# The 90th head of a score kernel is laid out anew, and its store becomes three DMAs

## The chip, the cores and the metric

The kernel runs on one core of one Trainium2 chip. Times are microseconds of device time. The number that counts is the median of the runs; a profile of one more execution shows where the time goes. A core has engines that work side by side: PE (matrix products), DVE and ACT (elementwise work, here mostly copies), POOL (GpSimd) and SP, which in this kernel only issues DMAs. ACT and POOL can issue DMAs too. A DMA's bytes are moved by 16 DMA engines that all issuers share.

## The reference

```python
def setup_inputs():
    batch, n_heads, seq, head_dim = 8, 12, 1024, 64
    ...
def reference(q, k):
    return np.einsum('bhid,bhjd->bhij', q, k).astype(np.float32)
```

For each of 96 heads (8 batches of 12) the product of q (1024 x 64) with k transposed (64 x 1024) is written out as 1024 x 1024 numbers in float32. That is 4 MiB of output for each head and 403 MB in all, against 50 MB of input.

## The kernel before

The heads are worked in blocks of 2, 2, 4, 8, 8 and six times 12 heads (`sizes`). For a block, q and k are loaded (`Block.load`, L73, or head by head in `load_head`, L84), cast to half precision by POOL (`cast_rows`, L97, and `cast_quads`, L127), and transposed, so that the 64 numbers of a row lie along the partitions: by PE and a copy in the first two blocks (`transpose_rows`, L151 and L154), by DVE in the others (`transpose_quads`, L145). While one block's heads are computed, the next block is transposed and the one after that cast and loaded. The last block has no next one, so nothing of that kind lies beside its twelve heads, the 85th to the 96th.

`scores` computes one head. It takes an output tile `o_sb` of 128 partitions x 8 rows x 1024 numbers (32 KB per partition) from a pool of three buffers. Partition p holds rows 8p to 8p+7 of the result. In each of four steps PE makes two of these rows for all partitions: four products of 64 x 128 weights with 64 x 512 numbers of k (L171), into a PSUM tile of 128 x 2048. There are two such tiles. ACT copies each to `o_sb` (L181); only in the very first head, where the tiles are half as large, does DVE take every other copy (L179). After the fourth copy SP issues one DMA for the whole head (L185). It reads 32 KB from each of 128 partitions and writes 4 MiB to one stretch of memory.

A head's first copy has to wait until the store of three heads earlier has landed, since it takes over that store's buffer. PE fills the two PSUM tiles ahead of the copies. `pin` keeps all instructions of an engine in the order in which the program makes them, so the queues of PE, ACT, DVE, POOL and SP run as the code is written: SP's queue holds the stores one after another, ACT's the copies and, in earlier blocks, the loads.

`in_pool` has two buffers of 24 KB per partition that hold the loads of the larger blocks; `half_pool` has five small half-precision tiles. After the last block has been cast and transposed, neither pool is used any more.

Of the kernel before, what the change touches and what calls it, by code (L numbers as in the profile page):

```python
# [8 lines left out]
F16 = mybir.dt.float16  # L9
F32 = mybir.dt.float32  # L10
P = 128

@with_exitstack
def kernel(
# [6 lines left out]
    nc = tc.nc  # L21

    B, H, S, D = q.shape
    NT = S // P
    BH = B * H
# [5 lines left out]
    of = out.rearrange("b h i j -> (b h) i j")  # L31
# [3 lines left out]
    PE_BLOCKS = 2  # L35
    NMAX = max(sizes)
    CHUNK = 48 * 32

    consts = ctx.enter_context(tc.tile_pool(name="consts", bufs=1))
    ident = consts.tile([P, P], F16)  # L40

    in_pool = ctx.enter_context(tc.tile_pool(name="in_pool", bufs=2))
    half_pool = ctx.enter_context(tc.tile_pool(name="half_pool", bufs=5))
    tr_pool = ctx.enter_context(tc.tile_pool(name="tr_pool", bufs=2))
    out_pool = ctx.enter_context(tc.tile_pool(name="out_pool", bufs=3))

    pin = tc.keep_in_program_order

    def half_tile():
        half_sb = half_pool.tile([P, CHUNK], F16, tag="half")  # L50
        return half_sb

    class Block:
# [3 lines left out]
        def __init__(self, first, N, by_pe):  # L57
# [5 lines left out]
            self.halves = {}  # L63
            self.cut = max(1, self.R * 32 // CHUNK + (self.R * 32 % CHUNK > 0))

# [90 lines left out]
        def scores(self, n, side, ps_pool, w):  # L156
# [31 lines left out]
                )  # L188
            )

    blocks, first = [], 0
    for i, N in enumerate(sizes):
        blocks.append(Block(first, N, i < PE_BLOCKS))
# [4 lines left out]
    at = 0  # L198
# [13 lines left out]
    def next_load(eng):  # L212
        if stream:
            b, x = stream.pop(0)
            b.load(x, eng)
# [9 lines left out]
    def to_half(last):  # L225
        while casts:
            i, c = casts[0]
            if i > last or (blocks[i], c[0]) in stream:
                return
            blocks[i].cast_quads(*c)  # L230
            casts.pop(0)
# [6 lines left out]
    def block(i, heads, ps_pool, w):  # L238
        b = blocks[i]
        nxt = blocks[i + 1] if i + 1 < len(blocks) else None  # L240
        for n in heads:
            side = {}
            if nxt and nxt.by_pe:
                if n == 1:
                    side = {
                        u: [
                            lambda x=u // 2: nxt.transpose_rows(
                                x, ps_pool, nc.vector.tensor_copy
                            )
                        ]  # L250
                        for u in (1, 3)
                    }
            elif nxt:
                parts = nxt.chunks()
                some = [s for m, s in enumerate(parts) if m * b.N // len(parts) == n]
                side = {0: [lambda s=s: nxt.transpose_quads(*s) for s in some]}

            if n == LOADS.get(i, 6):
                side[1] = side.get(1, []) + [lambda: next_load(nc.scalar)] * 2
            b.scores(n, side, ps_pool, w)  # L260
            to_half(i + 2 + (n == b.N - 1))

    LOADS = {0: None, 1: None, 2: 1, 3: 4, 4: 4}
# [3 lines left out]
    with tc.tile_pool(name="first_pool", bufs=4, space=bass.MemoryType.PSUM) as pool:  # L267
        for x in range(2):
            blocks[0].transpose_rows(x, pool, (nc.vector.tensor_copy, nc.scalar.copy)[x])
        block(0, [0], pool, 1)  # L270
    po_pool = ctx.enter_context(
        tc.tile_pool(name="po_pool", bufs=2, space=bass.MemoryType.PSUM)
    )
    block(0, [1], po_pool, 2)
    for i in range(1, len(blocks)):
        if i + 1 < len(blocks):
            blocks[i + 1].alloc()
        block(i, range(blocks[i].N), po_pool, 2)
# [30 lines left out]
```

## Time and profile before

| | us |
|---|---|
| median of three runs | 1063.13 (1063.03 to 1064.67) |
| span of the profiled execution | 1061.8 |
| ACT busy in it | 697.6 |
| PE busy | 701.3 |
| DVE busy | 471.5 |
| POOL busy | 368.3 |
| one copy of 128 x 2048 by ACT | 1.860 |
| one product of 64 x 512 numbers by PE | 0.617 |

The span is the time from the first to the last instruction of the profiled execution. A page of the profile gives the busy time of the engines, the span in 40 slices, the DMA queues, the chain of work that ended last, the costliest groups of instructions by line, and the DMAs by the line that issues them. A busy share says little by itself: an engine that isn't on the chain can idle for nothing. The DMA row of the slices is the mean over all 16 DMA engines, so a slice in which one of them works alone looks almost empty. In the list of groups, "x96" counts instructions, and the number behind the bar is their total busy time, then the mean of one in nanoseconds.

### The profile page before, as it was taken

The page shows a single profiled execution, that of the slowest core. Times are in us where ns is not written, and L with a number is a line of the kernel's source. Part 1 is how long each engine was busy: PE and PEld are TensorE (multiplying, and loading weights), DVE is VectorE, ACT ScalarE, POOL GpSimd, SP SyncE. Part 2 cuts the span into 40 slices and gives each one's busy share as a digit, 9 for nine tenths or more (in the row PEclk, how much of TensorE's full clock was granted, in tenths as well). Part 3 has the DMA queues.
Part 4 walks back from the last instruction along what each step waited for, and adds up shares of the span by engine and source line. Part 5 has one row for each costly group of instructions (what it writes and reads, how often), then busy time and mean ns, then how long its engine had stood idle before and what let it go on. Part 6 is the DMA issues. An engine that isn't in the chain of part 4 may idle for free.

```text
span 1061.8 us, 4282 instructions
## 1 busy us (share of the span) xinstructions
PE 701.3 (66%) x1568; PEld 241.6 (23%) x1568; DVE 471.5 (44%) x75; ACT 697.6 (66%) x386; POOL 368.3 (35%) x286
## 2 busy tenths in 40 slices
PE   6866755755677367773677836777367777778770
PEld 2322211211222122221222212222122222222220
DVE  2999601991696007960079600795007950000000
ACT  4856745755777366774677746777467777777771
POOL 6959128607630463303733046330463200000000
DMA  9999999999999999999999999999999999999997
GB/s 385 428 429 435 433 431 435 435 422 440 428 430 432 432 430 432 435 422 429 431 433 431 415 436 431 433 435 422 428 434 435 434 432 432 434 433 427 434 431 311
DMA packets 17588, 453.25 MB, mean 427 GB/s; under 512 B 1952, under 2 KB 1952, under 8 KB 2976
## 3 DMA queue, kind: packets, MB, share of 16 engines
q1 hardware_dynamic: 14688, 406.85, 89.1%
q10 hardware_dynamic: 2880, 46.14, 10.4%
q8 instruction: 12, 0.20, 0.1%
q14 instruction: 8, 0.07, 0.0%
HBM read 50.33 MB, written 402.65 MB: 427 GB/s over the span
## 4 chain that ended last, share of the span: by engine, by line
DMA 70%; ACT 17%; PE 7%; DVE 2%; issue 1%; POOL 1%; ACTq 0%; SPq 0%
DMA out_dram<-o_sb 70%; ACT o_sb L181 17%; PE ps L171 7%; DVE qT L145 1%; DVE kT L145 1%; DMA early<-in_q_dram 0%; POOL half_sb L127 0%; PE ps L151 0%; POOL half_sb L97 0%; DVE kT L154 0%; DVE o_sb L179 0%; ACTq L181 0%; ACT kT L154 0%; SPq L84 0%; ACTq L73 0%
## 5 line engine op out<-in xcount | busy, mean ns | idle before, releaser
L181 ACT COPY o_sb<-ps 128x2048 f32<-128x2048 f32 (+1 forms) x384 | 695.3, 1860 | 334.7 <-DMA out_dram<-o_sb 298.4
L171 PE MATMUL ps<-kT,qT 64*128 64x512 f16 x1536 | 697.2, 617 | 329.4 <-ACT o_sb L181 325.6
L127 POOL CAST half_sb<-x_sb 32x1536 f16<-32x1536 f32 (+1 forms) x256 | 346.5, 1353 | 455.1 <-DMA x_sb<-in_q_dram 318.3
L171 PEld LDWEIGHTS <-qT 64*128 64x128 f16 x1536 | 238.4, 157 | 786.3 <-issue 781.9
L145 DVE STREAM_TRANSPOSE qT<-half_sb 128x1536 f16<-128x1536 f16 (+1 forms) x34 | 232.8, 7140 | 372.2 <-issue 372.2
L145 DVE STREAM_TRANSPOSE kT<-half_sb 128x1536 f16<-128x1536 f16 (+1 forms) x34 | 234.2, 7181 | 0.0
L127 POOL CAST half_sb<-early 32x1024 f16<-32x1024 f32 x16 | 16.5, 1033 | 4.0 <-DMA early<-in_q_dram 3.3
L151 PE MATMUL ps<-ident,half_sb 128*128 128x128 f16 x32 | 4.1, 309 | 6.7 <-POOL half_sb L97 6.1
L154 DVE COPY qT<-ps 128x1024 f16<-128x1024 f16 x2 | 2.4, 1224 | 12.3 <-PE ps L151 12.3
L179 DVE COPY o_sb<-ps 128x1024 f32<-128x1024 f32 x4 | 4.9, 1224 | 4.3 <-PE ps L171 4.3
L97 POOL CAST half_sb<-early 128x512 f16<-128x512 f32 x8 | 4.6, 613 | 4.1 <-DMA early<-in_q_dram 4.1
L151 PEld LDWEIGHTS <-half_sb 128*128 128x128 f16 x32 | 3.2, 139 | 8.6 <-POOL half_sb L97 6.5
L154 ACT ACT_TABLE_LOAD x1 | 1.3, 1283 | 5.8 <-DMA early<-in_q_dram 5.8
L154 DVE COPY kT<-ps 128x1024 f16<-128x1024 f16 x1 | 1.2, 1224 | 4.3 <-PE ps L151 4.3
L154 ACT COPY kT<-ps 128x1024 f16<-128x1024 f16 x1 | 1.0, 1012 | 1.2 <-PE ps L151 1.2
masks.py:199 POOL TENSOR_SCALAR_AFFINE_SELECT ident<-ident 128x128 f16<-128x128 f16 x1 | 0.3, 292 | 0.1
masks.py:197 POOL MEMSET ident<- 128x128 f16 x1 | 0.2, 204 | 0.3 <-POOLq L293 0.3
L293 POOL MEMSET const-float32-0.0<- 128x1 f32 x1 | 0.1, 98 | 0.2 <-issue 0.2
L293 POOL MEMSET const-uint8-127<- 128x1 uint8 x1 | 0.1, 101 | 0.0
L293 POOL MEMSET const-bfloat16-1.0<- 128x1 bf16 x1 | 0.1, 100 | 0.0
L293 POOL MEMSET const-float32-1.0<- 128x1 f32 x1 | 0.1, 98 | 0.0
## 6 DMA issues: line engine op xcount, KB each, us to landing
out_dram<-o_sb SPq DMA_DIRECT2D x96, 4096.0 KB, 21.8
x_sb<-in_q_dram ACTq DMA_DIRECT2D x6, 3072.0 KB, 22.8
x_sb<-in_k_dram ACTq DMA_DIRECT2D x6, 3072.0 KB, 39.6
x_sb<-in_k_dram ACTq DMA_DIRECT2D x2, 2048.0 KB, 22.2
x_sb<-in_q_dram SPq DMA_DIRECT2D x1, 2048.0 KB, 18.0
x_sb<-in_q_dram ACTq DMA_DIRECT2D x1, 2048.0 KB, 19.0
early<-in_k_dram ACTq DMA_DIRECT2D x4, 256.0 KB, 5.0
early<-in_q_dram SPq DMA_DIRECT2D x4, 256.0 KB, 4.7
```

The costliest lines, as they stand in the source:

```text
L97: nc.gpsimd.tensor_copy(out=self.rows[x][:, :, half], in_=self.raw[x][:, half * n : (half + 1) * n].rearrange("p (r d) -> p r d", d=D),)
L127: nc.gpsimd.tensor_copy(out=half_sb[q0 : q0 + 32].rearrange("p (r d) -> p r d", d=32), in_=raw[32 * b : 32 * b + 32, c * m : (c + 1) * m, h],)
L145: pin(nc.vector.transpose(out=dst, in_=src))
L151: pin(nc.tensor.transpose(t_ps[:, t], self.rows[x][:, t], ident))
L154: pin(copy(out=dst, in_=src))
L171: nc.tensor.matmul(ps[:, at : at + 512], qT[cs, g, w * u + tt], kT[cs, g, js],)
L179: pin(nc.vector.tensor_copy(out=dst, in_=ps))
L181: pin(nc.scalar.copy(out=dst, in_=ps))
L293: nc = _bacc.Bacc("TRN2", target_bir_lowering=False, num_devices=1)
```

## The change

One head of the last block, the 90th (`b.first + n == SPLIT`, with `SPLIT = BH - 7 = 89` counted from zero), is no longer computed by `scores` but by the new `split_scores`. It does the following.

- A tiny DMA, issued by GpSimd, copies a few numbers of the identity matrix from 5 partitions to a new tile `spare` that nothing reads.
- Rows 0 to 511 of the head are computed four to a partition, in two PSUM tiles, copied by ACT to the first half of `o_sb`, and stored by a DMA of SP's (128 partitions x 16 KB).
- Rows 512 to 1023 are seen as four groups of 128. Of each group the first 88 rows lie one to a partition on partitions 40 to 127 of a tile `rest`, taken from `in_pool`. They are computed in two more PSUM tiles whose weights are 128 rows wide and start 40 rows earlier, so that the row lands on its partition; ACT copies all 128 partitions. GpSimd stores partitions 40 to 127: 88 x 4 pieces of 4 KB.
- The last 40 rows of each group, 160 in all, go five to a partition on partitions 0 to 31 (eight partitions to a group). A small DVE copy sorts the 64 x 160 numbers of `qT` into a half-precision tile; PE makes the rows in three steps of two, two and one row (ten products of 32 columns of weights); DVE copies them to `low_sb`, in the other buffer of `in_pool`; SP stores 32 partitions x 20 KB.

In all, partitions 0 to 31 hold nine rows of the head, 32 to 39 four, and 40 to 127 eight. PE makes ten narrow products (32 columns of weights) beside the 16 of before. ACT's four copies keep their size. The DMAs of this head are three large ones and a tiny one, in place of one. All other heads stay as they were.

```diff
+    SPLIT = BH - 7
+    NEAR, FAR = 32, 40
...
+    spare = consts.tile([P, P], F16)
...
+    def split_scores(b, n, ps_pool):
+        half, g = divmod(n, b.N // 2)
+        cs = slice(half * D, (half + 1) * D)
+        qT = b.qT[cs, g * S : (g + 1) * S]
+        kT = b.kT[cs, g * S : (g + 1) * S]
+        dst = of[b.first + n]
+        o_sb = out_pool.tile([P, NT, S], F32, tag="out")
+        rest = in_pool.tile([P, NMAX * S // P * D], F32, tag="x")
+        thin = slice(0, 64)
+        pin(
+            nc.gpsimd.dma_start(
+                out=spare[:5, thin].rearrange("p (a x) -> p a x", a=2)[:, :, :16],
+                in_=ident[:5, thin].rearrange("p (a x) -> p a x", a=2)[:, :, :16],
+            )
+        )
+        def rows(to, count, weights, copy):
+            ps = ps_pool.tile([P, 2 * S], F32, tag="po")
+            for m, w in enumerate(weights):
+                for j in range(2):
+                    at = m * S + j * 512
+                    pin(
+                        nc.tensor.matmul(
+                            ps[:count, at : at + 512], w, kT[:, j * 512 : j * 512 + 512]
+                        )
+                    )
+            pin(copy(out=to, in_=ps[:count, : len(weights) * S]))
+        flat = o_sb.rearrange("p t j -> p (t j)")
+        first = qT[:, : 4 * P].rearrange("c (p t) -> c t p", t=4)
+        for u in (0, 2):
+            rows(flat[:, u * S : (u + 2) * S], P, [first[:, u], first[:, u + 1]], nc.scalar.copy)
+        pin(
+            nc.sync.dma_start(
+                out=dst[: 4 * P].rearrange("(p t) j -> p (t j)", t=4),
+                in_=flat[:, : 4 * S],
+            )
+        )
+        groups = dst[4 * P :].rearrange("(g x) j -> g x j", g=4)
+        for u in (0, 2):
+            starts = [4 * P + a * P - FAR for a in (u, u + 1)]
+            rows(rest[:, u * S : (u + 2) * S], P, [qT[:, at : at + P] for at in starts], nc.scalar.copy)
+        pin(
+            nc.gpsimd.dma_start(
+                out=groups[:, : P - FAR].rearrange("a p j -> p a j"),
+                in_=rest[FAR:, : 4 * S].rearrange("p (a j) -> p a j", a=4),
+            )
+        )
+        low_sb = in_pool.tile([P, NMAX * S // P * D], F32, tag="x")
+        last = qT[:, 4 * P :].rearrange("c (g x) -> c g x", g=4)[:, :, P - FAR :]
+        sorted_sb = half_tile()
+        last_sb = sorted_sb[cs, : 5 * NEAR].rearrange("c (t p) -> c t p", t=5)
+        pin(
+            nc.vector.tensor_copy(
+                out=last_sb.rearrange("c t (g r) -> c t g r", g=4),
+                in_=last.rearrange("c g (r t) -> c t g r", t=5),
+            )
+        )
+        for ts in ((0, 1), (2, 3), (4,)):
+            rows(low_sb[:NEAR, ts[0] * S : (ts[-1] + 1) * S], NEAR, [last_sb[:, t] for t in ts], nc.vector.tensor_copy)
+        pin(
+            nc.sync.dma_start(
+                out=groups[:, P - FAR :].rearrange("g (r t) j -> g r (t j)", t=5),
+                in_=low_sb[:NEAR, : 5 * S],
+            )
+        )
...
-            b.scores(n, side, ps_pool, w)
+            if b.first + n == SPLIT:
+                split_scores(b, n, ps_pool)
+            else:
+                b.scores(n, side, ps_pool, w)
```

## The prediction

> **What bounds the kernel now.** I read the page's slices and its chain of work first, then the issue table, then the windows over the last 20 us, then the chain and the ACT timeline around the 90th head. Heads are counted from one.
>
> ```profile
> span 1061.8 us, 4282 instructions
> ...
> DMA  9999999999999999999999999999999999999997
> ...
> DMA 70%; ACT 17%; PE 7%; DVE 2%; issue 1%; POOL 1%; ACTq 0%; SPq 0%
> ...
> out_dram<-o_sb SPq DMA_DIRECT2D x96, 4096.0 KB, 21.8
> ```
>
> The DMA engines are full in all slices but the last, and the chain runs from store to store. So the stores' bytes bound the kernel, and an edit can gain only where some of the 16 DMA engines are not full: in that last slice. The windows there (share of the 16 DMA engines in the column before the last; packets count where they start):
>
> ```profile
> 1040.00:1052.00 12.00, 0.00 (x0) 0.00 (x0) 0.00 (x0) 0.00 (x0) 0.00 (x0) 1.00 1.01 437
> 1052.00:1054.00 2.00, 0.00 (x0) 0.00 (x0) 0.00 (x0) 0.00 (x0) 0.00 (x0) 1.00 0.76 328
> 1054.00:1055.00 1.00, 0.00 (x0) 0.00 (x0) 0.00 (x0) 0.00 (x0) 0.00 (x0) 1.00 0.38 164
> 1055.00:1056.00 1.00, 0.00 (x0) 0.00 (x0) 0.00 (x0) 0.00 (x0) 0.00 (x0) 1.00 0.15 66
> 1056.00:1057.00 1.00, 0.00 (x0) 0.00 (x0) 0.00 (x0) 0.00 (x0) 0.00 (x0) 1.00 0.08 33
> 1057.00:1058.00 1.00, 0.00 (x0) 0.00 (x0) 0.00 (x0) 0.00 (x0) 0.00 (x0) 1.00 0.08 33
> 1058.00:1060.00 2.00, 0.00 (x0) 0.00 (x0) 0.00 (x0) 0.00 (x0) 0.00 (x0) 1.00 0.04 16
> ```
>
> From 1056 on one packet starts per microsecond: a single DMA engine works. The trace's packet and semaphore records, read one by one, say more. A store is 128 packets of 32 KB; each of 16 engines takes eight (1.213 us each, the next starting 4 ns before the end, so 1.209) and then marks its landing. The marks of two stores:
>
> ```
> 90th head, issued  980.68: first  994.42, last four  998.08  998.17  999.11 1002.44
> 96th head, issued 1039.36: first 1052.82, last four 1056.12 1056.26 1057.06 1060.86
> ```
>
> One engine is 3.80 us behind the next one at the end. It isn't one accident: the same lag is 2.18 in the store issued at 447.68, 2.79 in that of 692.22, 3.21 in that of 833.95. Over the last 65 us the late engine's packets average 1.221 us against 1.213 to 1.219 on the others; a store of eight costs it up to 0.1 us more. Traced packet by packet, each engine ends with the same bytes: it is slow, not overloaded. Its last store frees the final waits (SP waits 21.0 us for it), and the program ends 1.0 us later.
>
> **The change part by part.**
>
> *Shares.* A whole store gives each engine 8 partitions x 32 KB. Of the 90th head partitions 32-39 keep four rows of eight, 4 x 4 KB x 8 = 128 KB less, that is 4 packets' worth, 4 x 1.209 = 4.84 us; partitions 0-31 get one row more, 32 KB for each of four engines, +1.21 us; the others keep 256 KB. The trace shows that eight partitions make one engine's share of a 128-partition store. It has no DMA of 88 or 32 partitions and no store by GpSimd, and it never names an engine. I take it that eights of partitions stay shares of one engine, and that 32-39 belong to the late one; the other readings are rivals below. The late engine's last landing then goes to 1060.86 - 4.84 = 1056.02, and the end passes to the next latest. Unless that one is among the four with a row more, it is 1057.06: gain 3.80. If it is among them: 1057.06 + 1.21 = 1058.27, gain 2.59. If 1056.26 or 1056.12 is among them: about 1057.47, gain 3.39. Four of the fifteen others get the row, so the first bad case has some 0.27; I take 3.4.
>
> The Trainium skill ("DMA: Bandwidth & Descriptors", "Why a DMA increments its semaphore by 16 and not by 1") says that a DMA uses the largest number of engines up to 16 that divides both slowest dimensions: from SP the lowest-numbered, from GpSimd consecutive ones from a cursor that moves on. By it the 4x8x5120 store would use engines 0-3, the tiny five-partition copy would move the cursor by five and the 88-partition store use engines 5-15, which leaves out engine 4 (if the cursor starts at 0); the sum would be the same. No run here shows it yet.
>
> *Packet sizes.* The big store's 32 KB packets become 16, 20 and 4 KB ones. Loads show 2 KB in 81-84 ns, 8 KB in 309, 16 KB in 611: about 37 ns per KB and 7 ns per packet, less the 4 ns overlap. So 128 KB in 4 KB pieces is 32 x (7 + 148 - 4) = 4.83 us against 4.84: nothing. By the 2 KB row's upper value it would be 64 x 0.080 = 5.12, +0.28. I take 0.1 and keep both.
>
> *GpSimd's issue.* POOL's last cast ends at 832, so the tiny copy (10 pieces) and the store queue behind nothing. The time that POOL needs for 352 pieces of 4 KB isn't in the trace. Lower bound: SP's first issue at 0.73 and first packet at 1.76, 1.0 us. Upper: a small POOL MEMSET per piece, 352 x 0.1 = 35 us. Whatever it is, the engines then do the next head's store first, and nothing but the end waits for this landing. At the upper bound an engine idles between its half of this head and the next store (below): the one that lands at 1057.06 has finished its half 4.84 us before 998.7, at 993.8, and idles till 996.3, so it ends 2.5 us later and the gain falls to 1.3. I take the low end, since idle starts only after 8 us of delay for the fastest engine.
>
> *Compute.* Before, ACT's turn for this head runs 973.20 to 980.66 and a new turn starts when the store of three heads earlier lands:
>
> ```profile
> 973.20 3.63 ACT L181 COPY o_sb<-ps 128x2048 f32<-128x2048 f32 x2 [2.33 <-DMA out_dram<-o_sb]
> 977.02 3.63 ACT L181 COPY o_sb<-ps 128x2048 f32<-128x2048 f32 x2 [0.18 <-PE ps L171]
> 982.97 3.64 ACT L181 COPY o_sb<-ps 128x2048 f32<-128x2048 f32 x2 [2.32 <-DMA out_dram<-o_sb]
> ```
> ```profile
> L179 DVE COPY o_sb<-ps 128x1024 f32<-128x1024 f32 x4 | 4.9, 1224 | 4.3 <-PE ps L171 4.3
> ```
>
> ACT's four copies stay (1.82 us each). The first store goes out after two of them, at 976.9, 3.8 us earlier than the whole one did; GpSimd's after four, at 980.7. Ten matmuls (8 took 3.63: 4.5 us) and three DVE copies are added, all through the two PSUM buffers. A DVE copy of 1024 columns is 1.224 us, so 2.45, 2.45 and 1.22; DVE has no other work after 865 (its last transposes end there). The small half-precision copy, 160 columns, under 1.22 us by the same row, has no one ahead of it and runs early. Step by step: PE first tile 978.9-980.7, DVE to 983.2; second to 985.7; third to 986.9, when SP issues the third store. The next head's first tile gets its buffer at 985.7, is ready at 987.5, ACT's turn ends at 995.2, and its store is issued then instead of at 990.46: 4.7 us late, in SP's queue behind nothing. First packets at 996.3. Engines that finish the 90th head before that (the fastest, 994.4 - 0.4 = 994.0) idle up to 2.3 us; they lead by more, ending near 1055. The engine of 1057.06 finishes at 998.7 and doesn't idle; the relieved one at 1002.0 - 4.84 = 997.2, nor does it. The 92nd head's turn runs 995.2 to 1002.7, and engines need it at 1006: the delay is absorbed. In_pool's two buffers are free, their last casts being over.
>
> *Sum.* Span 1061.8 - 3.4 + 0.1 = 1058.5. The runs' median 1063.13 stands 1.3 above the span; the same shift gives 1059.8.
>
> **Rivals.**
>
> *The late engine isn't the relieved one* (0.15). Its landing stays 1060.86 and so does the time: 1063.1, or +1.2 if it is one of the four with a row more. For: no record has the engine's number. Against: the lag is lasting, so a fixed relief can meet it. A sentence of the Trainium skill ("DMA: Bandwidth & Descriptors", "Latency and other measured facts") has engines 7 and 15 as usually the slower ones, which would make this rival true; the trace can't say, and the skill ties it to stores by GpSimd, which the kernel before hasn't got.
>
> *The 88 partitions are dealt otherwise, six to an engine over sixteen* (0.07). Then the four engines have 128 + 160 + 96 = 384 KB, +4.84 us, and the late one 224 KB, -1.21, landing 1059.65; the four land between about 1058.9 and 1061.9. Time 1062 to 1064, about 1063.0. For: no such DMA is in the trace. (The same section on the semaphore of 16 names such an exception for GpSimd's direct copies.)
>
> *Slower: the eleven shares fall on another eleven engines* (0.09). The four then have 128 + 160 + 128 = 416 KB, +6.05 us, and the late engine isn't relieved. It decides once one of the four lands later than 1060.86 - 6.05 = 1054.81 without the change; seven of the other fifteen marks lie above that. With 1057.06 among them the end is 1063.1: 1065.4; with 1056.1, 1064.4.
>
> *Slower: the next head's store comes too late* (0.06). Each microsecond past an issue at 997.7 (2.5 us over my 995.2) makes the engine of 1057.06 idle and moves the end; past 1001.5 the gain is gone. That takes the three DVE copies at twice their row. Ten microseconds late costs 1063.13 + 10 - 6.3 = 1066.8. Against: nothing else is queued on DVE.
>
> **How the numbers follow.** The forecast has 0.63. That the late engine is the relieved one no row can carry; this chance is a judgement and the weakest step. Its own range is 1059.2 (gain 3.8) to 1061.8 (gain 1.3). The whole range goes down to 1058.5, if the unprofiled lag is larger (the relief ends at 4.84), and up to 1063.7, which takes in the first two rivals. 0.2% is 2.1 us, about what a measurement of this kernel can tell from no change. Faster: 0.63 less the cases with under 2.1 us of gain, 0.60; slower, most of the last two rivals, 0.13; same 0.27.
>
> **What would show it.** Right: in the last windows no stretch of several microseconds with a DMA share near 0.06; the last store's latest mark within 1.3 us of the next; the 91st head's store issued near 995 and the 96th's earlier than 1039.4; a POOL queue moving about 1.4 MB. Wrong: one engine still 3 us behind the rest (first rival), four engines 4 to 6 us behind (second, third), or a dip of the DMA share near 990-1000 on all engines (fourth).

## The result and the profile after

The median rose from 1063.31 us (six runs of the kernel before, 1063.03 to 1064.67) to 1070.14 us (six runs, 1066.70 to 1071.47). The ratio is 1.0056, with a 95% interval of 1.0043 to 1.0069. The prediction was 1059.8 us, range 1058.5 to 1063.7: the time went the other way, by 6.8 us, and lies outside the range.

The profiled execution after the change took 1071.47 us, with a span of 1069.4. From its page come the span, the slices' DMA and GB/s rows, the queue that GpSimd feeds, the chain by engine, and the issues of three of the four kinds of stores (size, then microseconds from issue to landing; the 640 KB of `low_sb` are not on the page):

```profile
span 1069.4 us, 4314 instructions
...
DMA  9999999999999999999999999999999999999996
GB/s 385 434 434 432 432 427 435 431 433 427 433 436 425 432 433 435 433 421 432 434 431 432 426 431 431 434 431 423 427 433 434 432 436 434 430 431 416 362 427 270
...
q0 software_dynamic: 560, 1.44, 0.5%
...
DMA 68%; ACT 17%; PE 8%; DVE 2%; issue 1%; POOL 1%; ACTq 0%; SPq 0%
...
out_dram<-o_sb SPq DMA_DIRECT2D x95, 4096.0 KB, 21.8
...
out_dram<-o_sb SPq DMA_DIRECT2D x1, 2048.0 KB, 24.9
out_dram<-rest POOLq DMA_DIRECT2D x1, 1408.0 KB, 46.9
```

The DMA row still reads 9 in every slice but the last, so by that row nothing happened. The GB/s row has the loss: the 37th and 38th slices (962 to 1016 us) hold 416 and 362 where other slices hold about 432. The engines are as busy as before and move less. The windows around the 90th head show where it begins (start and end, length, the busy time of PE, of PE's weight loads, of DVE, ACT and POOL, then granted clock, DMA share and GB/s):

```profile
978.00:984.00 6.00, 4.85 (x11) 1.42 (x11) 3.65 (x2) 2.17 (x2) 0.80 (x1) 1.00 1.00 426
984.00:987.00 3.00, 2.12 (x6) 0.82 (x6) 1.96 (x2) 0.17 (x1) 0.00 (x0) 1.00 0.97 389
987.00:990.00 3.00, 2.71 (x8) 0.95 (x7) 0.00 (x0) 3.00 (x2) 0.00 (x0) 1.00 0.94 348
990.00:993.00 3.00, 2.82 (x8) 0.96 (x7) 0.00 (x0) 2.82 (x3) 0.00 (x0) 1.00 1.09 298
993.00:996.00 3.00, 3.00 (x8) 1.06 (x7) 0.00 (x0) 2.78 (x2) 0.00 (x0) 1.00 0.93 259
996.00:999.00 3.00, 2.78 (x8) 0.93 (x7) 0.00 (x0) 2.82 (x3) 0.00 (x0) 1.00 1.10 337
999.00:1002.00 3.00, 2.81 (x7) 0.95 (x6) 0.00 (x0) 2.96 (x2) 0.00 (x0) 1.00 0.99 326
1002.00:1008.00 6.00, 5.58 (x14) 1.96 (x13) 0.00 (x0) 5.64 (x4) 0.00 (x0) 1.00 1.03 406
...
1058.00:1060.00 2.00, 0.00 (x0) 0.00 (x0) 0.00 (x0) 0.00 (x0) 0.00 (x0) 1.00 0.46 197
1060.00:1062.00 2.00, 0.00 (x0) 0.00 (x0) 0.00 (x0) 0.00 (x0) 0.00 (x0) 1.00 0.23 98
1062.00:1064.00 2.00, 0.00 (x0) 0.00 (x0) 0.00 (x0) 0.00 (x0) 0.00 (x0) 1.00 0.08 33
1064.00:1068.00 4.00, 0.00 (x0) 0.00 (x0) 0.00 (x0) 0.00 (x0) 0.00 (x0) 1.00 0.04 16
```

From 984 on the share stays near 1 while the rate falls to 259 GB/s. The last two lines show that one engine still works alone at the end, as it did before the change. The packet records, counted where they lie rather than where they start, give the size of the loss:

```
GB/s in 3 us from   984  987  990  993  996  999 1002 1005 1008 1011 1014 1017
before              432  432  431  427  429  432  432  432  432  432  432  432
after               408  377  296  271  301  324  387  396  405  421  426  425
```

Against 432 the row of after lacks 5.2 us of all 16 engines (the sum of 3 x (432 - x) / 432 over its twelve windows). Single packets show how: one of 32 KB took up to 4.756 us (1.213 before), of 20 KB a median of 1.37 and up to 2.6 (0.761 where undisturbed), of 16 KB up to 2.29 (0.611), of 4 KB up to 0.84 (0.159). The landing marks of the last store show how this reaches the end:

```
96th head, before: first 1052.82, last four 1056.12 1056.26 1057.06 1060.86
96th head, after:  first 1057.27, last four 1062.39 1062.44 1062.85 1067.72
```

The second-last mark is 5.79 us later, close to the 5.2 us that all engines lost, and the last one's lag behind it went from 3.80 to 4.87 instead of vanishing: 5.79 + 1.07 = 6.86 us, most of the 7.6 us between the two profiled spans; the rest lies behind the last mark. (The medians differ by 6.8, but the profiled execution is the slowest of the six, so that the two figures nearly agree is chance.) The compute side did what it should. This is the timeline of after, without PE's lines (start, length, engine, line, operation):

```profile
972.67 3.63 ACT L222 COPY o_sb<-ps 128x2048 f32<-128x2048 f32 x2 [2.31 <-DMA out_dram<-o_sb]
976.33 0.33 SPq L234 DMA_DIRECT2D out_dram<-o_sb  x1
976.54 3.63 ACT L222 COPY rest<-ps 128x2048 f32<-128x2048 f32 x2 [0.23 <-PE ps L218]
980.35 5.61 DVE L222 COPY low_sb<-ps 32x2048 f32<-32x2048 f32 x3 [116.19 <-PE ps L218]
980.48 0.80 POOL L249 DMA_DIRECT2D out_dram<-rest  x1 [148.29 <-ACT rest L222]
985.99 0.78 SPq L272 DMA_DIRECT2D out_dram<-low_sb  x1
...
994.31 0.34 SPq L189 DMA_DIRECT2D out_dram<-o_sb  x1
```

The three stores were issued at 976.33, 980.48 and 985.99, and the 91st head's at 994.31 (990.46 before), each behind nothing else in its queue.

### The profile page after: what moved, and what is told of

Read it like the earlier page. It is cut to its first block, busy times and chain, and to the rows that moved or that the text cites. A ratio compares the mean times of both kernels' runs of the same rounds, so it can differ in the third digit from the quotient of the medians.

```text
span 1069.4 us, 4314 instructions
## 1 busy us (share of the span) xinstructions
PE 705.6 (66%) x1578; PEld 242.7 (23%) x1578; DVE 477.1 (45%) x79; ACT 697.2 (65%) x386; POOL 369.8 (35%) x288
## 4 chain that ended last, share of the span: by engine, by line
DMA 68%; ACT 17%; PE 8%; DVE 2%; issue 1%; POOL 1%; ACTq 0%; SPq 0%
DMA out_dram<-o_sb 68%; ACT o_sb L185 17%; PE ps L175 8%; DVE qT L149 1%; DVE kT L149 1%; DVE low_sb L222 0%; DMA early<-in_q_dram 0%; POOL half_sb L131 0%; PE ps L218 0%; PE ps L155 0%; ACT rest L222 0%; ACT o_sb L222 0%; POOL half_sb L101 0%; DVE o_sb L183 0%; DVE kT L158 0%
## 5 line engine op out<-in xcount | busy, mean ns | idle before, releaser
L185 ACT COPY o_sb<-ps 128x2048 f32<-128x2048 f32 (+1 forms) x380 | 687.6, 1859 | 339.4 <-DMA out_dram<-o_sb 295.9
L222 DVE COPY low_sb<-ps 32x2048 f32<-32x2048 f32 (+1 forms) x3 | 5.6, 1916 | 116.2 <-PE ps L218 116.2
L218 PE MATMUL ps<-kT,half_sb 64*32 64x512 f16 x10 | 4.6, 616 | 0.8 <-DVE low_sb L222 0.6
L222 ACT COPY o_sb<-ps 128x2048 f32<-128x2048 f32 x2 | 3.6, 1868 | 2.3 <-DMA out_dram<-o_sb 2.3
L222 ACT COPY rest<-ps 128x2048 f32<-128x2048 f32 x2 | 3.6, 1868 | 0.2 <-PE ps L218 0.2
## 6 DMA issues: line engine op xcount, KB each, us to landing
out_dram<-rest POOLq DMA_DIRECT2D x1, 1408.0 KB, 46.9
```

What stands on the lines that cost most here:

```text
L185: pin(nc.scalar.copy(out=dst, in_=ps))
L218: nc.tensor.matmul(ps[:count, at : at + 512], w, kT[:, j * 512 : j * 512 + 512])
L222: pin(copy(out=to, in_=ps[:count, : len(weights) * S]))
```

## The experiments

Seven readings had to be told apart. The letters in the expectations stand for them; in words (the diffs show the lines that matter, not whole edits):

- the late engine is not the one that the change relieves (rival B);
- G: GpSimd's queue, or its packets' alternation with SP's, slows the engines;
- W: the 4 KB pieces, strewn over memory, slow the writes;
- P: packets stretch when an engine reads partitions that a whole store gives to another engine. In its first form an engine's own partitions are eight neighbours, as the prediction took them; in its second, P4, they are two groups of four, 32 partitions apart;
- M: packets stretch where the blocks are written to memory in another order than that of a whole store;
- N: packets stretch in any store on fewer than 16 engines;
- the 91st head's store came too late (excluded by the timeline above).

P4's dealing is what the Trainium skill ("DMA: Bandwidth & Descriptors", "The descriptor swizzle") states for a 128-partition transfer: engine 8 x (p >> 6) + ((p >> 2) & 7) has partition p, so that engine 0 has 0-3 and 32-35, engine 4 has 16-19 and 48-51. No record names the partitions of a packet, so which engine reads which partitions is inferred in every run below.

**1. Which engine is late.** The trace doesn't name DMA engines. The kernel before gets 15 tiny DMAs of SP's of 1 to 15 partitions, two behind each store from the 85th head on; each leaves a short packet on so many engines.

```diff
+            for j in (2 * at + 1, 2 * at + 2):
+                if 1 <= j <= 15:
+                    m = 67 if j == 1 else 32 + 2 * j
+                    c = 80 * j
+                    pin(nc.sync.dma_start(out=tags[0][:j, c : c + m], in_=ident[:j, :m]))
```

> The kernel before, with fifteen tiny marker DMAs of SP's in the last block (two behind each store from the 85th head on): one of 1 partition, one of 2, and so on to 15, each with a row length of its own (134 B, then 64 + 4j B). Nothing else changes; about 3 MB/1000 of traffic, so the time should stay within 2 us. Each marker is on as many DMA engines as it has partitions, and if these are always the lowest-numbered, the engines that carry the marker of j partitions but not that of j - 1 are number j - 1. Theory A (the relieved share was that of the late engine, and the relief was eaten by slower packets): the engine that ends 3 to 4 us after the others is number 4, so it carries the markers of 5 to 15 partitions. Rival B (the late engine isn't the relieved one): it carries another set; if it is one of numbers 0 to 3, it got a row more instead.

Measured: 1063.86 us, beside 1063.15 for the kernel before. The fifteen sets of engines lie one inside the next, so each engine gets a number, its rank in that nesting. The ends of their last data packets:

```
engine   0       1       2       3       4       5       6       7
     1053.13 1055.04 1053.33 1052.54 1060.73 1055.25 1056.40 1052.59
engine   8       9      10      11      12      13      14      15
     1055.17 1057.22 1058.32 1053.24 1055.26 1052.91 1054.10 1052.99
```

Number 4 is the late one, as the prediction took it; rival B falls. The Trainium skill's section on the semaphore of 16 (same page, "Why a DMA increments its semaphore by 16 and not by 1") has SP's smaller DMAs on the lowest-numbered engines; the nesting of the sets agrees. The Trainium skill's "Latency and other measured facts" (same page) calls engines 7 and 15 the usually slower ones: here they are among the four earliest.

**2 to 4. A store split by partitions, by queue, by piece size.** Three variants of the kernel before change one thing each in the 90th head. In `mixmap` the store is cut at partition 32, both parts by SP, with the same bytes for every engine:

```diff
+                for ps in (slice(32, P), slice(0, 32)):
+                    pin(nc.sync.dma_start(out=dst[ps], in_=src[ps]))
```

> The kernel before, with the 90th head's store split by partitions into two of SP's, 32 to 127 and 0 to 31, all in 32 KB pieces: each of 16 engines should take six packets of the first and two of the second, so the shares stay eight packets for each engine, but an engine reads other partitions than in a whole store. Theory P (packets stretch when engines read partitions out of their usual pattern, and several meet in one part of SBUF): packets of 32 KB over 1.5 us in this store and a dip in GB/s, the time 1 to 5 us longer. Theory W (the 4 KB pieces strewn over the head's memory slow the writes) and theory G (a store by GpSimd slows the others): no stretch, the time within 1 us of before.

In `gphalf` the rows are halved instead, and GpSimd stores the second half of every partition:

```diff
+                for eng, c in ((nc.sync, 0), (nc.gpsimd, 1)):
+                    js = slice(c * 4 * S, (c + 1) * 4 * S)
+                    pin(eng.dma_start(out=dst[:, js], in_=src[:, js]))
```

> The kernel before, with the 90th head's store split into two halves of four rows a partition (128 partitions x 16 KB each), the first by SP and the second by GpSimd. Layout, shares and compute stay. Theory G (a store by GpSimd slows the others, or comes late): packets beside it stretch and the time grows by 1 to 5 us. Theories P and W: within 1 us of before.

In `strided_sp` rows 512 to 1023 lie in four groups of 128, one row of a group to a partition, and SP stores 128 x 4 pieces of 4 KB from all partitions:

```diff
+        groups = dst[4 * P :].rearrange("(a p) j -> p a j", a=4)
...
+            nc.sync.dma_start(
+                out=groups,
+                in_=rest[:, : 4 * S].rearrange("p (a j) -> p a j", a=4),
+            )
```

> The changed kernel without its shift of shares: the 90th head's first 512 rows four to a partition, the other 512 as four groups of 128 rows, one row of each group on every partition; both stores by SP, 128 x 16 KB and 128 x 4 pieces of 4 KB. No work by GpSimd, no DVE copies, every engine keeps 256 KB. Theory W (the strewn 4 KB pieces slow the writes): the pieces take well over 0.16 us each, a dip in GB/s, 1 to 5 us longer. Theories P and G: within 1 us of before.

| run | us | ratio to before |
|---|---|---|
| `mixmap` | 1074.66 (1070.11 to 1081.47) | 1.0112 [1.0069, 1.0155] |
| `gphalf` | 1063.68 | 1.0006 [0.9997, 1.0016] |
| `strided_sp` | 1064.30 | 1.0008 [0.9998, 1.0017] |

The same two windows of the three, in this order (the columns as above):

```profile
990.00:996.00 6.00, 1.83 (x5) 0.60 (x4) 0.00 (x0) 0.00 (x0) 0.00 (x0) 1.00 0.96 273
996.00:1002.00 6.00, 2.22 (x6) 0.83 (x6) 0.00 (x0) 3.96 (x3) 0.00 (x0) 1.00 1.01 276
```
```profile
990.00:996.00 6.00, 2.09 (x5) 0.64 (x4) 0.00 (x0) 0.18 (x1) 0.00 (x0) 1.00 1.01 429
996.00:1002.00 6.00, 3.82 (x9) 1.40 (x9) 0.00 (x0) 5.75 (x4) 0.00 (x0) 1.00 1.04 442
```
```profile
990.00:996.00 6.00, 3.68 (x10) 1.27 (x8) 0.00 (x0) 3.69 (x3) 0.00 (x0) 1.00 0.98 399
996.00:1002.00 6.00, 5.78 (x13) 1.88 (x12) 0.00 (x0) 5.59 (x4) 0.00 (x0) 1.00 1.09 457
```

Only the cut by partitions has the dip, with full engines, packets of 32 KB up to 5.04 us long, and no GpSimd, no small piece and no shift of work in it. It is 11.5 us slower by the medians, where 1 to 5 were expected under P. Part of that comes later: the stretched stores hold their buffer, ACT waits 10.0 us for it, the 93rd head's store goes out at 1022.82 (1010.02 before), and between 1017 and 1026 the 16 engines lose 1.3 us for want of work. (In the last pair the low first window is a matter of where packets are counted: the two together hold 428.) GpSimd's queue (G) and the strewn pieces (W) cost nothing that can be measured here, each on its own.

**5 and 6. The changed kernel with one of its two odd stores.** `no_low` leaves out the third store, `no_gp` GpSimd's two DMAs; the rows concerned, 160 and 352, stay unwritten, all computing stays.

```diff
-        pin(
-            nc.sync.dma_start(
-                out=groups[:, P - FAR :].rearrange("g (r t) j -> g r (t j)", t=5),
-                in_=low_sb[:NEAR, : 5 * S],
-            )
-        )
```

> The changed kernel with the third store left out (SP's, 32 partitions x 20 KB, on four engines): 160 rows of the 90th head aren't written, everything else stays. 0.66 MB less to move, which alone is 1.5 us over 16 engines, or 6 us for the four that carry it. Theory P1 (the four-engine store reads other engines' parts of SBUF and stretches the packets): the dip in GB/s after 986 is gone, packets keep 1.21 us, the time is 1060 to 1062. Theory P2 (GpSimd's 88-partition store does it): the dip remains, from the first software packet on, and the time is over 1064.

```diff
-        pin(
-            nc.gpsimd.dma_start(
-                out=groups[:, : P - FAR].rearrange("a p j -> p a j"),
-                in_=rest[FAR:, : 4 * S].rearrange("p (a j) -> p a j", a=4),
-            )
-        )
```

> The changed kernel with GpSimd's two DMAs left out: 352 rows of the 90th head aren't written, 1.44 MB less (3.4 us over 16 engines), the tiny copy isn't made. Theory P1: the dip remains from the first 20 KB packet on, with packets of 1.2 us and more where 0.76 is the length of one alone. Theory P2: no dip, 20 KB packets of 0.76 us. If both stores stretch packets, both runs show part of it.

`no_low` took 1066.64 us (1.0033 [1.0021, 1.0045]), `no_gp` 1065.29 (1.0023 [1.0007, 1.0039]), both slower than before though they write less. In both the rate falls, first `no_low`, then `no_gp`:

```profile
984.00:990.00 6.00, 4.51 (x11) 1.72 (x11) 2.50 (x2) 2.63 (x2) 0.00 (x0) 1.00 0.98 375
990.00:996.00 6.00, 5.81 (x14) 2.05 (x13) 0.00 (x0) 5.59 (x4) 0.00 (x0) 1.00 0.83 272
```
```profile
984.00:990.00 6.00, 4.51 (x12) 1.76 (x12) 2.38 (x2) 2.75 (x2) 0.00 (x0) 1.00 0.94 401
990.00:996.00 6.00, 5.81 (x15) 2.04 (x14) 0.00 (x0) 5.59 (x4) 0.00 (x0) 1.00 0.76 295
```

Part of this is idle engines, which have less to do (shares of 0.83 and 0.76), but packets stretch too: 16 KB up to 2.0 us in `no_low`, 20 KB 1.24 to 1.82 us on one engine in `no_gp`. So either store does it alone. (In `no_low` G and W come together, GpSimd issuing strewn 4 KB pieces; no run has that pair with every partition read by its usual engine.) The last engine's lag was 1.75 us in the profile of `no_low` and 4.87 in that of `no_gp`, as in the changed kernel: in these executions the large lag comes with the third store. It isn't steady either: `tags_no_gp` below, `no_gp` with markers, has 2.22.

**7. The order in memory, and eights.** `dramperm` is the kernel before, except that the 90th head's store takes its partitions in groups of eight and writes a group's eight blocks 512 KB apart (the rows land in other places of that head).

```diff
+                dst = of[self.first + n].rearrange("(r g t) j -> g r (t j)", g=16, r=8)
+                src = o_sb.rearrange("p t j -> p (t j)")
+                pin(nc.sync.dma_start(out=dst, in_=src))
```

> The kernel before, with the 90th head's rows written in another order of its 32 KB blocks: partition 8g + r writes block 16r + g in place of 8g + r, by one store of SP's (16 groups x 8 partitions x 32 KB), so the 90th head's rows land in other places than the reference's. The DMA engines' shares are eight packets each. Theory P (where in SBUF an engine reads decides) with groups of eight partitions as an engine's own: no stretch, within 1 us of before. Theory M (where in memory the engines write decides: in the split by partitions each engine also wrote other blocks): packets stretch, 1 us or more longer.

Measured: 1076.57 us (1.0108 [1.0070, 1.0145]). The windows of its profile have the deepest dip of all:

```profile
984.00:990.00 6.00, 5.21 (x12) 1.87 (x12) 0.00 (x0) 5.82 (x4) 0.00 (x0) 1.00 1.16 289
990.00:996.00 6.00, 2.06 (x5) 0.63 (x4) 0.00 (x0) 0.15 (x1) 0.00 (x0) 1.00 0.88 210
```

If eight neighbours were an engine's own partitions, nothing should have stretched here, under P in its first form. That form fell. P4 and M were left, since this run changes the order in memory as well as the dealing by fours. P4 gives a size, too: engines that start together on eights meet two by two on eight of the sixteen pairs of fours, and if two engines on one pair share what one engine gets alone, the rate is half of 432, an estimate of 216 GB/s. The packet records of 987 to 993 have 204 to 214.

**8. The same shares, dealt by fours.** `aligned` gives every engine the bytes that the change gives it, and from partitions that P4 calls its own: engine 4's (16-19 and 48-51) keep four rows, engines 0 to 3 get one row more, on 0-15 and 32-47. The second half of the head goes out in eight DMAs, each in groups of four partitions.

```diff
+        second = dst[4 * P :].rearrange("(e x) j -> e (x j)", e=8).rearrange(
+            "e (b r y) -> b e r y", b=4, r=4
+        )
...
+                    out=second[bb, lo:hi],
+                    in_=rest[p + 4 * lo : p + 4 * hi, : 4 * S],
...
+        thin(0)
+        piece(nc.sync, 0, 0, 4)
+        piece(nc.sync, 1, 0, 4)
+        piece(nc.gpsimd, 0, 5, 8)
+        piece(nc.gpsimd, 2, 0, 8)
+        thin(64)
+        piece(nc.gpsimd, 1, 5, 8)
+        piece(nc.gpsimd, 3, 0, 8)
...
+                    out=extra[bb], in_=rest[32 * bb : 32 * bb + 16, 4 * S : 5 * S]
```

Here `piece(engine, b, lo, hi)` stores partitions 32b + 4lo to 32b + 4hi - 1, and `thin` is the change's tiny copy, which moves GpSimd's cursor on by five engines.

> The changed kernel's shares with another dealing of partitions. The 90th head's first half is stored as in the change. Its other 512 rows are stored by eight DMAs in which a DMA engine always takes four neighbouring partitions: engine e the partitions 4e to 4e+3 and 32+4e to 35+4e (e up to 7), or 64+4(e-8) and 96+4(e-8) onwards (e from 8). Partitions 16-19 and 48-51, engine 4's by this rule, keep four rows of eight; engines 0 to 3 store one row more on partitions 0-15 and 32-47; all others 256 KB. So engine 4 is relieved by 128 KB and each of engines 0 to 3 gets 32 KB more, as in the change. Theory P4 (in a whole store an engine owns those two fours of partitions, and packets stretch when an engine reads another's): no dip in GB/s, packets of 16 KB at 0.61 us, no engine several microseconds late at the end, and a time of 1059.5 to 1061.5. Rival N (any store on fewer than 16 engines, or writes that leave the usual order of memory, stretch the packets): a dip as in the change, 1064 or more.

Measured: 1062.34 us (11 runs, 1060.20 to 1064.08), ratio 0.9992 [0.9983, 1.0001]. Its windows, the same ones and the end:

```profile
984.00:990.00 6.00, 5.52 (x13) 1.88 (x12) 0.00 (x0) 5.82 (x4) 0.00 (x0) 1.00 0.99 415
990.00:996.00 6.00, 4.29 (x10) 1.42 (x9) 0.00 (x0) 4.30 (x3) 0.00 (x0) 1.00 1.02 419
996.00:1002.00 6.00, 5.59 (x14) 1.92 (x13) 0.00 (x0) 5.60 (x5) 0.00 (x0) 1.00 1.04 446
```
```profile
1053.00:1054.00 1.00, 0.00 (x0) 0.00 (x0) 0.00 (x0) 0.00 (x0) 0.00 (x0) 1.00 0.61 262
1054.00:1055.00 1.00, 0.00 (x0) 0.00 (x0) 0.00 (x0) 0.00 (x0) 0.00 (x0) 1.00 0.46 197
1055.00:1056.00 1.00, 0.00 (x0) 0.00 (x0) 0.00 (x0) 0.00 (x0) 0.00 (x0) 1.00 0.15 66
1056.00:1057.00 1.00, 0.00 (x0) 0.00 (x0) 0.00 (x0) 0.00 (x0) 0.00 (x0) 1.00 0.00 0
```

No dip, a median of 0.615 us for 16 KB (three of 248 packets over 0.79, the longest 0.938), and no engine alone at the end: the last five marks are 1056.25 to 1056.91. This profile is of the fastest of the eleven runs, and the median lies above the 1059.5 to 1061.5 expected. N falls, since these stores are on three, four and eight engines. With the same bytes for each engine, seven DMAs more and ACT's four copies of the same size, it lies 7.8 us below the changed kernel.

**9 and 10. The markers again, in the changed kernel and in `no_gp`.** The edit is that of run 1, with markers of 1 to 6 partitions from the 92nd head on in `tags_after`, and of 1 to 15 from the 81st on in `tags_no_gp` (again without the 352 rows of GpSimd's store). In the first:

```diff
+    TAG0 = 91
...
+            for j in range(2 * at + 1, 2 * at + 1 + 2):
+                if 1 <= j <= 6:
```

> The changed kernel with six tiny marker DMAs (of 1 to 6 partitions, two behind each store from the 92nd head on), which tell engines 0 to 5 by their numbers after the disturbed stretch; up to 2 us of change. Theory P4: engine 4, though it has 128 KB less, isn't the last any more or ends with the rest; the last one is an engine from 0 to 3 that read two fours of others while it had 160 KB of five-row pieces. Rival: engine 4 is still last, so its relief was lost on itself.

> The changed kernel without GpSimd's two DMAs (352 rows unwritten), with fifteen marker DMAs before the 90th head. The five-row store's packets can be followed here engine by engine. Theory P4: engine 0 reads the fours of 0 and 1, engine 1 those of 2 and 3, engine 2 those of 4 and 5, engine 3 those of 6 and 7; so engine 2 meets the late engine 4 and its packets stretch from the first on, to 1.2 us or more where the others keep 0.76 until the next head's store begins near 996. Rival: the stretched one is another engine, or all four alike.

`tags_after` took 1072.48 us. Engines 0 to 5 ended at 1058.66, 1059.87, 1069.03, 1061.13, 1060.34 and 1061.84, and no other one later than 1062.14. So engine 4 is no longer late but in the middle of the pack, and the last engine is another: number 2, 6.9 us behind the next. Of the third store it reads partitions 16-23, which P4 gives to engines 4 and 5.

`tags_no_gp` (1067.83 us) came out in part only. Engine 2's eight packets of 20 KB took 761, 1467, 1504, 1509, 1315, 1584, 1505 and 1768 ns, long from about the time that engine 4 came to its 16 KB packets. But the first was not stretched, and engine 3, the last one there at 1064.69, had packets of 761 ns until 997.5 and of 1.24 to 1.82 us after that, once the next head's whole store ran. Which pairs of engines meet and when is thus only partly accounted for.

**11 and 12. What the relief is worth.** `aligned_flat` deals the second half by fours and moves no rows between engines; `aligned_again` is `aligned` once more.

```diff
+        thin(0)
+        piece(nc.sync, 0, 0, 8)
+        piece(nc.sync, 1, 0, 8)
+        piece(nc.gpsimd, 2, 0, 8)
+        thin(64)
+        piece(nc.gpsimd, 3, 0, 8)
```

> The dealing by fours of the run aligned, without its shift of shares: the 90th head's second half is stored by four DMAs of 32 partitions on eight engines each (0-31 and 32-63 by SP on engines 0 to 7, 64-95 and 96-127 by GpSimd on engines 8 to 15, with tiny copies of eight partitions ahead), four rows on every partition, so each engine has 256 KB as before. Theory P4: no dip although the DMAs use eight engines and two queues, engine 4 still 3 to 4 us behind at the end, the time within 1 us of before (1063.3). Then what aligned gains over this run is the relief of engine 4 alone, 2 to 3 us by the marks, 1 us or more by its first measurement. Rival N (DMAs on fewer than 16 engines stretch packets): a dip, 1065 or more.

> The kernel of the run aligned once more, beside its control on the same chip: its eleven times lay between 1060.2 and 1064.1, wider than those of before. Expected by theory P4: 1060.5 to 1062.5, 1 to 2.5 us under aligned_flat and 0.5 to 2.5 under before. If the relief is worth nothing outside the profile: the same as aligned_flat within 0.7 us.

`aligned_flat`: 1064.37 us (1063.68 to 1065.01), ratio 1.0010 [1.0001, 1.0019]. `aligned_again`: 1062.30 us (1060.40 to 1064.32), ratio 0.9989 [0.9980, 0.9998]. By the medians the dealing without relief costs about 1 us, and the version with the relief is 1064.37 - 1062.30 = 2.1 faster than that. That these 2.1 us are engine 4's lag isn't shown: `aligned_flat` was expected to have that engine 3 to 4 us behind at the end, and the last two marks of its profile are 1060.88 and 1061.09, only 0.21 apart. The version dealt by fours with the relief lies about 1 us of 1063 below the kernel before; the interval excludes no change in the second set (0.9980 to 0.9998), and not quite in the first (0.9983 to 1.0001).

**13. Partitions or memory.** In `seven` each engine writes one orderly run of seven blocks to memory, from seven neighbouring partitions (an eighth of the head is left unwritten).

```diff
+                dst = of[self.first + n].rearrange("(g r t) j -> g r (t j)", g=16, r=8)
+                src = o_sb.rearrange("p t j -> p (t j)")
+                pin(nc.sync.dma_start(out=dst[:, :7], in_=src[:112]))
```

> The kernel before, with the 90th head's store leaving out one block of 32 KB in eight: 16 groups of 7 partitions (0 to 111), each group written in order to its own 256 KB of memory. Partition 7g + r writes block 8g + r, so the head's rows land in other places than the reference's and an eighth isn't written. Each engine takes seven packets, and each engine's stretch of memory is one run of 224 KB in order, as orderly as in a whole store. Theory P (reading partitions out of an engine's own stretches the packets): 32 KB packets of 2 us and more, a dip of GB/s, 1066 or more. Theory M (writing memory in another order does it): no packet over 1.5 us, no dip, 1061 to 1063.5 (an eighth of a store is 1.2 us less).

Measured: 1074.11 us (1.0114 [1.0093, 1.0136]), with an eighth less of that head to write. Its windows have the dip again:

```profile
984.00:990.00 6.00, 5.41 (x13) 1.89 (x13) 0.00 (x0) 5.76 (x4) 0.00 (x0) 1.00 1.05 350
990.00:996.00 6.00, 1.85 (x5) 0.62 (x4) 0.00 (x0) 0.00 (x0) 0.00 (x0) 1.00 1.05 311
996.00:1002.00 6.00, 1.87 (x5) 0.73 (x5) 0.00 (x0) 3.63 (x2) 0.00 (x0) 1.00 0.88 309
```

Packets of 32 KB took up to 5.26 us, although each engine's memory lay in one piece. M falls. That the engines' runs lie 256 KB apart in memory here, and 128 KB in a whole store by P4, doesn't do it either: in `aligned` and `aligned_flat` neighbouring engines also write 256 KB apart, without a dip (429, 418 and 440 GB/s in `aligned_flat`'s same three windows). What is left is which partitions an engine reads.

## Why the prediction was wrong

The step that failed, in its own words: "I take it that eights of partitions stay shares of one engine, and that 32-39 belong to the late one; the other readings are rivals below." The second half of it held in its outcome alone: engine 4 was the late one (`tags`) and the change left it out, so that it ended with the others (`tags_after`). The prediction had no row for that and said so; that it came out is luck. By P4, partitions 32-39 are engine 0's and engine 1's in a whole store. The first half took "eight partitions make one engine's share" to mean eight neighbours. In a whole store an engine's share is, as far as the runs tell, two fours, 32 partitions apart (`dramperm` and `seven` stretch, `aligned` and `aligned_flat` don't). A DMA of 32 partitions on four engines, or of 88 on eleven, is dealt in runs of eight, so these engines read partitions that in the stores before and behind belong to others, and while both dealings were under way packets took up to four times as long, and those of 4 KB up to five times. The rule of the fours stands in the Trainium skill's section on the swizzle, cited above; the prediction had not weighed it, although it speaks against this change. The "other readings" were readings of who gets how many bytes. That the same number of bytes could take longer because of where it is read was in none of them.

Point by point:

- *The bound.* Right: the DMA engines set the end, and one engine's lag closes the run. But a lag is only the last few microseconds of it; the sum took the rate of the other 1050 us as untouched, and 5.2 us were lost there.
- *Shares.* The bytes per engine came as the prediction had them, and so did the dealing that it cites from the Trainium skill's section on the semaphore of 16: GpSimd's store is 352 packets of 4 KB (11 x 32), with 160 packets of 4 bytes beside them (5 x 32); the tiny copy, at 836.8, is five packets of 64 bytes and eleven of 8; the third store is 32 packets of 20 KB. The counts fit eleven engines, five others and four. The term's size, 3.4 us, was too large even without the collision, if the 2.1 us between the medians of `aligned_flat` and `aligned_again` are what the relief is worth. It was made from a lag of 3.80 in one execution, and the lag isn't that steady: 2.41 in `tags`, 0.21 in `aligned_flat`.
- *Packet sizes.* Taken as 0.1 us. As sizes alone this is right (`strided_sp`, 1.0008 with an interval that holds 1); undisturbed packets of 4, 16 and 20 KB took 0.159, 0.611 and 0.761 us.
- *GpSimd's issue.* POOL was busy for 0.80 us, and the first 4 KB packet came 5.6 us after the issue, at 986.06, between the bounds of 1.0 and 35 and below the 8 us from which it was to matter. A store by GpSimd costs nothing in itself (`gphalf`). This one's landing took 46.9 us, since on an engine its small packets alternate with the 32 KB ones of the stores behind it; nothing but the end waits for it, as the prediction said.
- *Compute.* Right: the 91st head's store was issued at 994.31 (predicted 995.2), DVE's copies ended at 985.96 (986.9), and no engine ran dry for it.
- *The rivals.* The two slower ones that were named did not occur: one engine ended late in `tags_after`, not four, and engine 4 was not it, so the eleven shares are where the prediction meant them; and the next head's store was in time. The sign of a dip "of the DMA share near 990-1000 on all engines" was set for the wrong thing: the share kept up and the rate did not.

Left open: what it is that two engines share when they read one another's partitions; the runs show only that packets stretch and which dealing avoids it. The lengths point at two engines taking turns at one rate, which no run proves: in `no_low`, of 127 packets of 4 KB that took over 1.15 times 0.159 us, 65 took 1.9 to 2.1 times that. Nor has any run dealt whole fours to the wrong engines; that each pair of fours belongs to one engine of its own, and not only that an engine has to read in fours, rests on engine 2 in `tags_no_gp`, on the 216 GB/s estimated for `dramperm` and on the dealing cited above. Why engine 4 is slow at all wasn't tried. The range of the times of `aligned` (1060.2 to 1064.3 over both sets) is wider than that of the kernel before, and its cause isn't known.

## What to carry to other kernels

When the DMA engines bound a kernel, look at the GB/s row and at packet lengths, since the busy share counts a stretched packet as work. Before a full-width store is cut by partitions, ask which partitions each DMA engine reads in the pieces and in the stores around them; a cut along the rows of every partition, or along the engines' own groups of four, kept the rate here, and a cut at partition 32 or 40 lost more than the 2 us that could be won. A lag at the end of one trace is a poor measure of what can be won: it was 3.8 us in the profile of the kernel before, and the version that relieved the late engine was 2.1 us faster than the one that didn't, about 1 us faster than the kernel before.

## What the hardware showed unexpectedly

- One store cut at partition 32, with equal bytes for all engines, lowers the rate of the 16 engines together from 432 to about 275 GB/s for 12 us and costs 11.5 us by the medians, 1.1% (`mixmap`). The whole 4 MiB take 9.7 us at 432 GB/s.
- The disturbance lasts while the oddly dealt stores are under way. In the changed kernel the third store's last mark is at 1009.56 and GpSimd's at 1027.39; the five windows from 1005 to 1020 still hold 396 to 426 GB/s, and from 1029 on the rate is 432 again. In `mixmap` the last stretched packet starts at 1012.34, and the two parts have landed by 1015.24.
- Of 16 DMA engines, number 4 was the slow one, 2.4 us behind the next in `tags`, at the same number of bytes but for the markers; 7 and 15 were among the earliest.
- What an issue costs isn't set by its pieces: GpSimd's with 352 pieces took 0.80 us, SP's with 32 pieces 0.78 and SP's with 128 pieces 0.33.
